# Encoder block on one core: branch A's exponentials left in PSUM, the first token block's keys regrouped in blocks of 128, half of the final scalings placed later

## The chip, the cores and the metric

One Trainium2 chip, one of its cores. The metric is device time of one execution in microseconds (us); lower is better. The kernel before ran three times: 1910.77 us is the median (1910.61 to 1911.93).

## What is computed

One layer of a hybrid encoder over two token groups with the same weights: `x_sample` (512 tokens) and `x_prompt` (2048 tokens), width 1024. 16 learned meta tokens stand ahead of each group. Cut to what matters here:

```python
u = rms_norm(h, norm_g)
qa, ka, va, za, qb, kb, vb, zb, ga, gb = split(u @ w_in)          # 42 tiles of 128 output columns
# branch A, 8 heads of 64: the tokens are a grid 64 wide; a query sees 8 rows x 16 columns and 16 meta keys
logits = concat([s_win * scale + bias, s_meta * scale]);  p = softmax(logits);  o_a = p @ v
# branch B, 8 query heads and 2 key heads: +-128 tokens and the meta keys, with a sink in the denominator
merged = sigmoid(ga) * ((o_a * silu(za)) @ w_proj_a) + sigmoid(gb) * ((o_b * silu(zb)) @ w_proj_b)
y = rms_norm(h + merged @ w_out, final_g)                          # meta tokens dropped
```

Everything is float32. A matrix product is made of three: each operand is split in a high part that TensorE's float32r holds and a low remainder, and high x high, high x low and low x high are added up (`mm3`, L134).

## The kernel before

The 2560 tokens are 5 windows of 512 (w = 0 is the sample, w = 1 to 4 the prompt). The first half, up to about 990 us, makes the input projection: window 4 tile by tile (`alone`, L679), the two pairs of windows by a seven-product scheme (`pairs`, L786). What the attention needs is written to DRAM: queries, keys, values, gates. The values of branch A go to `va_d`, ordered by blocks of 8 grid columns (`put_v`, L611); the meta values go to `vrow_d` (`put_v_meta`, L622), which is zeroed first from the tile `zr` (L625 to L630, run in the first half when the meta values of head pair 0 are ready). In this half TensorE's and SyncE's (SP's) order is that of the program; SP issues nearly all DMAs, one after the other.

The second half runs window by window: branch A's attention (32 units, `unit_a`, L980), then branch B's (`unit_b`, L1057). A unit is one head and one group g of 16 query columns, that is 128 queries. It goes through five steps that the main loop interleaves, so that four units are under way at a time:

1. loads (SP).
2. scores: two matmuls into a PSUM bank `s` of the pool `ps_s` (2 banks); VectorE (DVE) adds the bias and takes the maximum (`scores_max`, L950); ScalarE (ACT) writes the exponentials to the SBUF tile `pr`, regrouped by blocks of 8 columns, and sums them (`exps`, L959).
3. `normalise` (L967): `pr` times the inverse sum, in place; on ACT for g = 1, on DVE for the other three groups.
4. TensorE transposes `pr` block by block into a bank `tp` of the pool `ps_p` (3 banks); ACT and DVE split it in `ph` and `pl`.
5. TensorE multiplies `ph` and `pl` by the values into the bank `oa` (lists `A_ORDER` and `A_PRODUCTS`, L63 and L64). A block holds 8 columns of all key rows and one more row for the meta keys: 8 x (rows + 1) keys. In window 0 there are 8 rows, so a block has 72 keys; a head has 3, 4, 4 and 3 blocks to transpose in its four groups and 0, 6, 4 and 6 products.

Between these steps TensorE takes "dense" work in small pieces (`phases`, L1356): while branch A of window w runs, `dense_pb(w - 1)` and the first half of `dense_out(w - 1)`; while branch B runs, the second half of `dense_out(w - 1)`, `dense_pa(w)` and, filled in between, `dense_fin(w - 1)` (L1247). The last makes the RMSNorm factor `rbs` and then multiplies the eight result tiles `hT` by it on GpSimd (POOL), each followed by its store. In window 0 the dense work is the gate columns of window 4 (`gate`, L281). In this half TensorE's order is the program's; the other engines' order is the scheduler's. POOL also makes the low parts of the weights (`split_part`, L188, through `lo_eng`), POOL's share of `dense_pb` (L1219 and L1223) and `y` and its low part (`y_split`, L973).

Between the halves, `open_weights` (L937) sets `lo_eng` to POOL and splits the first weights of the second half; `prep_last(False)` (L299) makes window 4's operand `u` (L316 on ACT, L317 on DVE); and `finals` (L1396) are the last three sums of the seven-product scheme, on DVE, read out of PSUM banks that the second half's pools take over.

Of the kernel before, what the change touches and what calls it, by code (L numbers as in the profile page):

```python
# [70 lines left out]

def v_block(b):

    return b % 2 * 4 + b // 2
# [13 lines left out]
def encoder_block(ctx: ExitStack, tc: tile.TileContext, xT, x_end, w_in, w_pa, w_pb, w_o, norm_g, final_g,  # L88
# [15 lines left out]
    va_d = [dt(f"va{p}", [2, TOK // GRID_W * 8, 8, P]) for p in range(4)]  # L104
    vrow_d = [dt(f"vrow{p}", [8, 8, 2, P]) for p in range(4)]
# [192 lines left out]

    def prep_last(meta):  # L299
# [6 lines left out]
        for k in range(0, KT, 2):  # L306
# [601 lines left out]
    with tc.tile_pool(name="sp", bufs=1, reuse_waits="tile") as sp:  # L908
# [6 lines left out]
        next(steps)  # L915
        begun = beside(firsts, raws, wts, (own, (9, 14)), 0, steps, [2, 20, 27, *(28 + 27 * i // 10 for i in range(16))])
# [20 lines left out]
    def open_weights():  # L937
        nonlocal weights
        lo_eng[0] = nc.gpsimd
# [27 lines left out]
    def normalise(pr, rd, on_act=False):  # L967
        if on_act:
            nc.scalar.mul(pr, pr, rd)
        else:  # L970
            nc.vector.tensor_scalar(pr, pr, rd, None, ALU.mult)

    def y_split(br, w, p, y32, eng=nc.gpsimd):  # L973
# [4 lines left out]
        eng.tensor_sub(yl[:, p, :], y32, f32(yh[:, p, :]))  # L978

    def unit_a(w, p, h, g, sh):  # L980
# [17 lines left out]
        if g == 0:  # L998
# [5 lines left out]
            move(v[8:kb], va_d[p][h, t0 // 8 : t0 // 8 + kb - 8])  # L1004
            move(v[:8], vrow_d[p][:, :, h])
# [7 lines left out]
        s = ps_s.tile([P, WTOK], F32, tag="s", name="s")  # L1013
# [12 lines left out]
        for i, b in enumerate(A_ORDER[g]):  # L1026
# [369 lines left out]
    for fn in finals:  # L1396
        fn()
# [167 lines left out]
```

## Time and profile before

| | |
|---|---|
| median of 3 runs | 1910.77 us |
| the profiled execution's own time | 1908.84 us |
| its span (first to last instruction) | 1906.5 us |
| TensorE busy | 1878.5 us (99%) |
| VectorE busy | 1320.3 us (69%) |
| ScalarE busy | 1147.6 us (60%) |
| GpSimd busy | 731.9 us (38%) |
| DMA | 423.78 MB, 222 GB/s over the span |

How to read it: the page and the views describe the profiled execution, whose own time is the span and 2.3 us around it. Matmuls overlap in the pipeline, so the duration of one is longer than the distance from its start to the next one's start; the distance is what a matmul costs. "Idle before" an instruction is time in which its engine had nothing to run, and the name behind the arrow is what ended it.

### The profile page before, as it was taken

The page shows a single profiled execution, that of the slowest core. Times are in us where ns is not written, and L with a number is a line of the kernel's source. Part 1 is how long each engine was busy: PE and PEld are TensorE (multiplying, and loading weights), DVE is VectorE, ACT ScalarE, POOL GpSimd, SP SyncE. Part 2 cuts the span into 40 slices and gives each one's busy share as a digit, 9 for nine tenths or more (in the row PEclk, how much of TensorE's full clock was granted, in tenths as well). Part 3 has the DMA queues.
Part 4 walks back from the last instruction along what each step waited for, and adds up shares of the span by engine and source line. Part 5 has one row for each costly group of instructions (what it writes and reads, how often), then busy time and mean ns, then how long its engine had stood idle before and what let it go on. Part 6 is the DMA issues. An engine that isn't in the chain of part 4 may idle for free.

```text
span 1906.5 us, 29720 instructions
## 1 busy us (share of the span) xinstructions
PE 1878.5 (99%) x9925; PEld 1599.4 (84%) x9925; DVE 1320.3 (69%) x2887; ACT 1147.6 (60%) x2515; POOL 731.9 (38%) x556
## 2 busy tenths in 40 slices
PE   8999999999999999999999999999999999999998
PEld 6998888888888888888878888888888888888886
DVE  8886455556477544445457788878987887888874
ACT  6454443434464444444356787797788788878932
POOL 2005342323103232323223335655844773585420
PEclk9999999999999999999999999999999999999999
DMA  7667554645296765644368877977986996697473
GB/s 261 218 190 293 175 198 165 218 174 177 83 353 218 239 210 194 194 138 160 105 207 289 254 217 261 294 223 242 319 270 185 307 316 217 197 326 252 124 289 141
DMA packets 223760, 423.78 MB, mean 222 GB/s; under 512 B 49640, under 2 KB 90808, under 8 KB 222072
## 3 DMA queue, kind: packets, MB, share of 16 engines
q1 hardware_dynamic: 223320, 421.88, 66.8%
q8 instruction: 79, 1.29, 0.3%
q14 instruction: 73, 0.60, 0.1%
q10 hardware_dynamic: 288, 0.01, 0.0%
HBM read 303.07 MB, written 118.74 MB: 221 GB/s over the span
## 4 chain that ended last, share of the span: by engine, by line
PE 75%; DVE 9%; ACT 6%; DMA 5%; issue 3%; POOL 2%; SPq 0%; ACTq 0%; DVEq 0%; POOLq 0%
PE pa L762 21%; PE pe L762 10%; PE pc L762 5%; PE mm L135 4%; PE mm L137 4%; PE mm L136 4%; PE tp L1027 2%; PE pso L137 2%; PE pso L135 2%; PE pso L136 2%; PE tp L1129 1%; PE oa L1044 1%; PE oa L1042 1%; DVE s L953 1%; DMA wo<-wos 1%
## 5 line engine op out<-in xcount | busy, mean ns | idle before, releaser
L190 POOL TENSOR_TENSOR wt<-wraw,wt 128x512 fp32r<-128x512 f32 x164 | 215.4, 1331 | 288.2 <-ACT wt L189 288.1
L762 PE MATMUL pa<-u,wt 128*128 128x512 f32 x1008 | 242.9, 390 | 0.0
L762 PE MATMUL pa<-u,x 128*128 128x512 f32 x984 | 237.8, 390 | 0.0
L189 ACT CAST wt<-wraw 128x512 fp32r<-128x512 f32 x312 | 177.9, 620 | 73.8 <-PE mm L137 37.6
L762 PEld LDWEIGHTS pa<-u,wt 128*128 128x128 f32 x1008 | 188.7, 188 | 39.0
L762 PEld LDWEIGHTS pa<-u,x 128*128 128x128 f32 x984 | 183.9, 188 | 38.1
L733 POOL TENSOR_TENSOR s<-wraw,raw 128x512 f32<-128x512 f32 x40 | 57.9, 1447 | 271.7 <-DVE x L190 271.7
L135 PE MATMUL mm<-u,wt 128*128 128x512 f32 (+2 forms) x416 | 151.6, 364 | 7.3 <-ACT u L316 7.3
L728 POOL TENSOR_TENSOR s<-raw 128x512 f32<-128x512 f32 x40 | 60.0, 1500 | 253.3 <-DMA raw<-in_w_in_dram 137.0
L136 PE MATMUL mm<-u,wt 128*128 128x512 f32 (+2 forms) x416 | 147.5, 355 | 1.5 <-DVE u L317 1.5
L137 PE MATMUL mm<-u,wt 128*128 128x512 f32 (+2 forms) x416 | 147.5, 355 | 0.8 <-DVE wt L190 0.8
L190 DVE TENSOR_TENSOR wt<-wraw,wt 128x512 fp32r<-128x512 f32 x148 | 104.6, 746 | 61.6 <-ACT wt L189 61.5
L762 PE MATMUL pe<-u,wt 128*128 128x512 f32 x504 | 121.9, 391 | 0.0
L762 PE MATMUL pc<-u,wt 128*128 128x512 f32 x504 | 121.1, 389 | 0.0
L1031 DVE TENSOR_TENSOR pl<-tp,ph 128x512 fp32r<-128x512 f32 (+7 forms) x160 | 98.8, 617 | 24.0 <-ACT ph L1030 22.3
L762 PE MATMUL pe<-u,x 128*128 128x512 f32 x480 | 115.3, 389 | 0.0
L960 ACT ACTIVATE pr<-s,nm 128x384 f32<-128x384 f32 (+5 forms) x160 | 91.3, 571 | 37.9 <-DVE nm L953 35.4
L762 PEld LDWEIGHTS pc<-u,wt 128*128 128x128 f32 x504 | 94.6, 188 | 19.6
L762 PEld LDWEIGHTS pe<-u,wt 128*128 128x128 f32 x504 | 94.2, 188 | 19.4
L741 POOL TENSOR_TENSOR s<-wraw,s 128x512 f32<-128x512 f32 x40 | 52.9, 1322 | 146.2 <-DVE wt L190 146.2
L1030 ACT CAST ph<-tp 128x512 fp32r<-128x512 f32 (+7 forms) x160 | 84.7, 529 | 38.7 <-PE tp L1027 36.5
L135 PE MATMUL pso<-mh,wt 128*128 128x512 f32 x256 | 107.1, 418 | 0.0
(238 smaller groups left out, 5050.7 us busy)
## 6 DMA issues: line engine op xcount, KB each, us to landing
wraw<-in_w_in_dram SPq DMA_DIRECT2D x86, 512.0 KB
qa<-evq SPq DMA_DIRECT2D x20, 1024.0 KB
raw<-in_w_in_dram SPq DMA_DIRECT2D x40, 512.0 KB
q<-qa SPq DMA_DIRECT2D x20, 1024.0 KB
wraw<-in_w_o_dram SPq DMA_DIRECT2D x32, 512.0 KB
kbt<-kb SPq DMA_DIRECT2D x32, 384.0 KB
qb<-evq SPq DMA_DIRECT2D x20, 512.0 KB
ka<-evk SPq DMA_DIRECT2D x20, 512.0 KB
```

Of the source, the lines that this page charges most:

```text
L135: nc.tensor.matmul(ps, wh, uh, start=first, stop=False)
L136: nc.tensor.matmul(ps, wh, ul, start=False, stop=False)
L137: nc.tensor.matmul(ps, wl, uh, start=False, stop=last)
L189: nc.scalar.copy(h, r)
L190: low[0] = (eng or lo_eng[0]).tensor_sub(l, r, f32(h)).ins
L728: eng.tensor_add(s1, a21, a22)
L733: eng.tensor_sub(s3, a11, a21)
L741: eng.tensor_sub(s4, a12, s2)
L762: nc.tensor.matmul(ps, wt[:, a, s], u[:, b, kk, :], start=first and kk == 0 and i == 0, stop=kk == 3 and i == 2, skip_group_check=True)
L960: nc.scalar.activation(out, s, AF.Exp, bias=nm, scale=-1.0, accum_out=sm)
L1030: nc.scalar.copy(ph_[:kb, a], tb)
L1031: nc.vector.tensor_sub(pl_[:kb, a], tb, f32(ph_[:kb, a]))
```

## The change

- **Exponentials in PSUM.** For branch A, `exps` writes back into the bank of the scores, in its order, instead of into `pr`. `normalise` reads that bank and writes `pr`, regrouped. The bank is held until then. Every third unit takes its score bank from `ps_p` (the pool of the transposes), the others from `ps_s`. Branch B keeps its form.
- **Window 0's key blocks.** `pr` holds the 16 meta probabilities (normalised by a second small instruction in each unit) and then the 64 keys of each 8-column block without a gap. It is cut in blocks of 128 keys, some of them overlapping (`A0_BLOCKS`): 2, 3, 3 and 2 to transpose in the four groups, and 0, 4, 4 and 4 products (`A0_PRODUCTS`). The values of window 0 get an array of their own, `va0_d`, laid out in six such blocks of up to 128 rows; `put_v` stores into it with four DMAs for each head pair where there were two, `put_v_meta` with three more, and a unit loads it with two DMAs as before.
- **Zeros.** A function `zero_rows` sets `zr` and stores zeros into `vrow_d` (4 DMAs) and `va0_d` (8 DMAs). It runs at the start, behind the loads of the first operands; the 4 DMAs in `put_v_meta` are gone.
- **Final scalings.** For windows 0, 1 and 2, `dense_fin` scales and stores the first four tiles `hT`; the other four are scaled and stored during the next `dense_pb`, behind its fourth step. Window 3's stay together.
- **Between the halves.** `lo_eng` becomes POOL only after the first weights of the second half are split, so DVE makes the low parts of those; and the DVE instructions of `finals` are queued behind the last L317 of `prep_last`.

The diff, cut to its core:

```diff
+A0_BEGIN = ((16, 0), (16, 0), (16, 0), (0, 192))
+A0_BLOCKS = (((0, 0), (80, 1)), ((16, 2), (144, 4), (0, 6)), ((16, 5), (0, 7), (144, 9)), ((0, 10), (80, 11)))
+A0_PRODUCTS = ((),
+               (("h", 0, P, 1, (0, 1)), ("h", 4, 80, 0, (0,)), ("l", 4, 80, 0, (0,)), ("l", 0, P, 1, (0, 1))),
+               (("h", 1, P, 4, (1, 2)), ("l", 1, P, 4, (1, 2)), ("h", 5, 80, 6, (1, 2)), ("l", 5, 80, 6, (1, 2))),
+               (("h", 2, P, 9, (2, 3)), ("h", 3, P, 11, (3,)), ("l", 3, P, 11, (3,)), ("l", 2, P, 9, (2, 3))))
...
+    va0_d = [dt(f"va0{p}", [2, P, 6, P]) for p in range(4)]
...
-                nc.vector.scalar_tensor_tensor(ul[:, k + j, :WTOK], xt[:, j, :], g, f32(h), ALU.mult, ALU.subtract)
+                scaled[0] = nc.vector.scalar_tensor_tensor(ul[:, k + j, :WTOK], xt[:, j, :], g, f32(h), ALU.mult,
+                                                           ALU.subtract).ins
...
-        if br == "a":
+        if br == "a" and w == 0:
+            for rows, k, y, b in (slice(64, P), slice(0, 3), 0, 0), (slice(0, 64), slice(1, 4), 64, 0), \
+                    (slice(64, P), slice(3, 4), 48, 3), (slice(0, 64), slice(0, 1), N_META, 4):
+                n = k.stop - k.start
+                move(va0_d[p][:, y : y + 64, b : b + n].rearrange("g p k f -> p g k f"), vn[rows, :, k])
+        elif br == "a":
...
+    def zero_rows():
+        zr = ev.tile([P, WTOK], F32, tag="t", name="zr", bufs=3)[:, :P]
+        nc.vector.memset(zr, 0.0)
+        for d, v in zip(vrow_d, va0_d):
+            move(d.rearrange("c b g f -> (c b g) f"), zr)
+            move(v[:, :48, 3].rearrange("g p f -> p g f"), zr[:48, None, :].broadcast_to([48, 2, P]))
+            move(v[:, N_META:80, 5].rearrange("g p f -> p g f"), zr[:64, None, :].broadcast_to([64, 2, P]))
...
-            if p == 0:
-                zr = ev.tile([P, WTOK], F32, tag="t", name="zr", bufs=3)[:, :P]
-                nc.vector.memset(zr, 0.0)
-                for d in vrow_d:
-                    move(d.rearrange("c b g f -> (c b g) f"), zr)
+            for y, b in (P - N_META, 3), (0, 4), (0, 5):
+                move(va0_d[p][:, y : y + N_META, b].rearrange("g p f -> p g f"), vm[:, :, 0])
...
         next(steps)
+        zero_rows()
         begun = beside(firsts, raws, wts, (own, (9, 14)), 0, steps, [2, 20, 27, *(28 + 27 * i // 10 for i in range(16))])
...
     def open_weights():
         nonlocal weights
-        lo_eng[0] = nc.gpsimd
         weights = Weights(srcs)
...
-            move(v[8:kb], va_d[p][h, t0 // 8 : t0 // 8 + kb - 8])
-            move(v[:8], vrow_d[p][:, :, h])
+            if w == 0:
+                move(v[:, :4], va0_d[p][h, :, :4])
+                move(v[:80, 4:6], va0_d[p][h, :80, 4:])
+            else:
+                move(v[8:kb], va_d[p][h, t0 // 8 : t0 // 8 + kb - 8])
+                move(v[:8], vrow_d[p][:, :, h])
...
-        s = ps_s.tile([P, WTOK], F32, tag="s", name="s")
+        turn[0] += 1
+        s = (ps_p.tile([P, WTOK], F32, tag="tp", name="s") if turn[0] % 3 == 0 else
+             ps_s.tile([P, WTOK], F32, tag="s", name="s"))
...
-        pr = at.tile([P, 2 * HALF], F32, tag="pr", name="pr", bufs=3)[:, :WTOK]
-        sm = sums_of()[:, :1]
-        exps(pr[:, :n].rearrange("p (b r c) -> p r b c", b=nb, c=8), sv.rearrange("p r (b c) -> p r b c", c=8), nm, sm)
-        yield
-        normalise(pr[:, :n], inverse(sm), on_act=g == 1)
+        sm = sums_of()[:, :1]
+        exps(s[:, :n], s[:, :n], nm, sm)
+        yield
+        pr = at.tile([P, 2 * HALF], F32, tag="pr", name="pr", bufs=3)[:, :WTOK]
+        rd = inverse(sm)
+        x, r0 = (A0_BEGIN[g][0], 1) if w == 0 else (0, 0)
+        normalise(pr[:, x : x + nb * 8 * (R - r0)].rearrange("p (b r c) -> p r b c", b=nb, c=8),
+                  sv[:, r0:].rearrange("p r (b c) -> p r b c", c=8), rd, on_act=g == 1)
+        if w == 0:
+            x, m0 = A0_BEGIN[g][1], META_COLS[(0, 0, 1, 2)[g]] - c0
+            normalise(pr[:, x : x + N_META], sv[:, 0, m0 : m0 + N_META], rd, on_act=g == 1)
...
-    def dense_fin(w):
+    def dense_fin(w, fs):
...
-        for f in range(KT):
+        yield from final_scale(w, range(fs))
+
+    def final_scale(w, fs):
+        for f in fs:
             hT = acc["h", w, f]
             with tc.issue_after(low[0]):
-                nc.gpsimd.tensor_mul(hT, hT, rbs)
+                nc.gpsimd.tensor_mul(hT, hT, acc["r", w])
...
-                yield from dense_pb(w - 1)
+                pb = dense_pb(w - 1)
+                yield from islice(pb, 4)
+                yield from with_fill(pb, final_scale(w - 2, range(KT // 2, KT)) if w > 1 else iter(()))
                 yield from dense_out(w - 1, range(0, 4))
...
-            yield from with_fill(pa, dense_fin(w - 1))
+            yield from with_fill(pa, dense_fin(w - 1, KT if w == NWIN - 1 else KT // 2))
...
+    lo_eng[0] = nc.gpsimd
...
-    for fn in finals:
-        fn()
+    with tc.issue_after(scaled[0]):
+        for fn in finals:
+            fn()
```

## Rows read from the trace of the kernel before

**Rows 1.** The page, first part: busy time, share of the span and instructions of each engine.

```profile
PE 1878.5 (99%) x9925; PEld 1599.4 (84%) x9925; DVE 1320.3 (69%) x2887; ACT 1147.6 (60%) x2515; POOL 731.9 (38%) x556
```

**Rows 2.** The view of waits, TensorE alone: who waited for whom; total us, times, longest us.

```profile
PE mm L135 <- ACT u L316: 7.3, 1, 7.3
PE psb L136 <- POOL yb L978: 2.9, 3, 1.3
PE psa L135 <- ACT rbs L1255: 2.6, 3, 0.9
PE mm L136 <- DVE u L317: 1.5, 1, 1.5
PE tp L1027 <- DVE pr L971: 1.4, 5, 0.5
```

**Rows 3.** The view by windows: the stretch from 985 to 1080 us (window 0's branch A) and from 1300 to 1400 us (end of window 1's branch B, then most of window 2's branch A): length, busy us and count of each engine, granted TensorE clock, DMA busy share, GB/s.

```profile
985.00:1080.00 95.00, 93.32 (x550) 79.82 (x550) 71.80 (x188) 62.98 (x152) 38.18 (x30) 1.00 0.84 272
1300.00:1400.00 100.00, 97.65 (x582) 83.34 (x582) 88.45 (x215) 75.92 (x173) 70.40 (x55) 1.00 0.92 298
```

**Rows 4.** The timeline of TensorE in window 0's branch A: start us, us, engine, line, operation, tile, shape, count.

```profile
997.33 0.49 PE L1027 MATMUL tp<-ident,pr 128*72 128x128 f32 x3
997.57 0.48 PE L135 MATMUL mm<-u,wt 128*128 128x512 f32 x1
...
999.27 0.60 PE L1027 MATMUL tp<-ident,pr 128*72 128x128 f32 x4
999.62 0.48 PE L135 MATMUL mm<-u,wt 128*128 128x512 f32 x1
...
1003.63 0.28 PE L1044 MATMUL oa<-pl,v 72*64 72x256 f32 x1
1003.75 0.29 PE L1015 MATMUL s<-kd,q 128*128 128x288 f32 x1
```

**Rows 5.** The view of groups by shape, TensorE: all transposes of window 0's branch A (72 keys each): busy us, mean ns of one, idle before.

```profile
L1027 PE MATMUL tp<-ident,pr 128*72 128x128 f32 x112 | 17.4, 272 | 0.0
```

**Rows 6.** The view of the tile `pr` (duration ns: least, median, most; first and last start; forms), and the view of groups by shape for VectorE (busy us, mean ns of one, idle before): branch A's normalisation in SBUF, and the bias-and-maximum instruction, which reads and writes PSUM, at 384 columns.

```profile
L971 DVE TENSOR_SCALAR pr<-pr,rd x120: 315/504/1608, 995.1 to 1741.0; 128x384 f32<-128x384 f32 x40, 128x288 f32<-128x288 f32 x24, 128x216 f32<-128x216 f32 x16, 128x512 f32<-128x512 f32 x16
...
L971 DVE TENSOR_SCALAR pr<-pr,rd 128x384 f32<-128x384 f32 x40 | 31.6, 791 | 0.6
L953 DVE CUSTOM_DVE_ANT_0 s<-s,ba 128x384 f32<-128x384 f32 x48 | 26.6, 554 | 3.4 <-PE s L1016 3.4
```

**Rows 7.** The timeline of all engines around 1336 us: GpSimd, two normalisations, TensorE.

```profile
1334.49 2.73 POOL L190 TENSOR_TENSOR wt<-wraw,wt 128x512 fp32r<-128x512 f32 x2 [0.49 <-ACT wt L189]
1334.61 1.45 DVE L971 TENSOR_SCALAR pr<-pr,rd 128x512 f32<-128x512 f32 x1
...
1336.12 0.66 PE L1027 MATMUL tp<-ident,pr 128*128 128x128 f32 x4 [0.39 <-DVE pr L971]
...
1339.45 0.42 DVE L971 TENSOR_SCALAR pr<-pr,rd 128x384 f32<-128x384 f32 x1
```

**Rows 8.** The timeline of GpSimd at the end of window 1's branch B, and the TensorE instruction that waited for the last of it.

```profile
1317.30 5.05 POOL L1259 TENSOR_TENSOR hT<-hT,rbs 128x512 f32<-128x512 f32 x4 [2.46 <-ACT rbs L1255]
...
1326.24 5.27 POOL L1259 TENSOR_TENSOR hT<-hT,rbs 128x512 f32<-128x512 f32 x4
...
1337.17 1.29 POOL L978 TENSOR_TENSOR yb<-y,yb 128x512 fp32r<-128x512 f32 x1
...
1338.51 0.50 PE L136 MATMUL psb<-yb,wt 128*128 128x512 f32 x1 [0.81 <-POOL yb L978]
```

**Rows 9.** The timeline of all engines around 1316 us: a normalisation, the copy of `rbs` on ScalarE, and TensorE's wait for the bank that it frees.

```profile
1312.31 1.38 DVE L971 TENSOR_SCALAR pr<-pr,rd 128x384 f32<-128x384 f32 x1
...
1316.64 0.57 ACT L1255 COPY rbs<-rs_rb 128x512 f32<-128x512 f32 x1
...
1317.27 0.50 PE L135 MATMUL psa<-ya,wt 128*128 128x512 f32 x1 [0.93 <-ACT rbs L1255]
```

**Rows 10.** The timeline of all engines between the halves: the first four L317, the last two, the matmul that waited for the first of those, the last of `finals`' reads of PSUM, and the second half's first scores.

```profile
980.65 2.74 DVE L317 SCALAR_TENSOR_TENSOR u<-xt,ng,u 128x512 fp32r<-128x512 f32 x4 [8.47 <-ACT u L316]
...
988.52 1.40 DVE L317 SCALAR_TENSOR_TENSOR u<-xt,ng,u 128x512 fp32r<-128x512 f32 x2
989.32 0.51 PE L136 MATMUL mm<-u,wt 128*128 128x512 f32 x1 [1.48 <-DVE u L317]
...
990.18 0.68 DVE L263 TENSOR_TENSOR eva<-pb,u 128x512 f32<-128x512 f32 x1
...
990.96 0.34 PE L1015 MATMUL s<-kd,q 128*128 128x216 f32 x1 [0.20 <-PE mm L137]
```

**Rows 11.** The start: the view of the tile `zr` (issue time of its stores in ns on SP: least, median, most), and the timeline: an early memset, SP's issue of the fifth weights, their cast, and the sums that the next two windows' operands hang on.

```profile
L131 SPq DMA_DIRECT2D vrow<-zr x4: 417/570/1135, 104.1 to 106.5; - x4
...
0.95 0.06 DVE L339 MEMSET sq<- 128x5 f32 x1
...
19.01 0.43 SPq L131 DMA_DIRECT2D wraw<-in_w_in_dram  x1
...
28.75 1.13 ACT L189 CAST wt<-wraw 128x512 fp32r<-128x512 f32 x2
...
41.89 1.92 PE L410 MATMUL fin_v<-ones,rsp 128*128 128x1 f32 x16 [0.23 <-DVE rsp L405]
```

**Rows 12.** The view of waits, SP alone: the longest of those for GpSimd's low part in `dense_pb`; total us, times, longest us.

```profile
SPq L131 <- POOL ml L1223: 34.5, 20, 4.4
```

More of the change, by code (lines that the diff above doesn't have):

```diff
@@ L965, in inverse, with normalise @@
         return rd
-    def normalise(pr, rd, on_act=False):
+    def normalise(out, pr, rd, on_act=False):
         if on_act:
-            nc.scalar.mul(pr, pr, rd)
+            nc.scalar.mul(out, pr, rd)
         else:
-            nc.vector.tensor_scalar(pr, pr, rd, None, ALU.mult)
+            nc.vector.tensor_scalar(out, pr, rd, None, ALU.mult)
     def y_split(br, w, p, y32, eng=nc.gpsimd):
@@ L978, in y_split @@
         eng.tensor_sub(yl[:, p, :], y32, f32(yh[:, p, :]))
+    turn = [0]
     def unit_a(w, p, h, g, sh):
@@ L1018, in unit_a @@
         nm = scores_max(s, n, bias[:, b0 : b0 + n])
+        sm = sums_of()[:, :1]
+        exps(s[:, :n], s[:, :n], nm, sm)
+        yield
         pr = at.tile([P, 2 * HALF], F32, tag="pr", name="pr", bufs=3)[:, :WTOK]
-        sm = sums_of()[:, :1]
-        exps(pr[:, :n].rearrange("p (b r c) -> p r b c", b=nb, c=8), sv.rearrange("p r (b c) -> p r b c", c=8), nm, sm)
-        yield
-        normalise(pr[:, :n], inverse(sm), on_act=g == 1)
+        rd = inverse(sm)
[5 more added lines that the diff above has]
+            normalise(pr[:, x : x + N_META], sv[:, 0, m0 : m0 + N_META], rd, on_act=g == 1)
         yield
         tp = ps_p.tile([P, WTOK], F32, tag="tp", name="tp")
-        for i, b in enumerate(A_ORDER[g]):
-            nc.tensor.transpose(tp[:kb, i * P : (i + 1) * P], pr[:, b * kb : (b + 1) * kb], ident)
-        a = slice(A_FIRST[g], A_FIRST[g] + 2 * nb - 1, 2)
-        tb = tp[:kb, : nb * P].rearrange("p (b t) -> p b t", t=P)
+        if w == 0:
+            kb, blocks = P, A0_BLOCKS[g]
+            products = A0_PRODUCTS[g]
+        else:
+            blocks = [(b * kb, A_FIRST[g] + 2 * i) for i, b in enumerate(A_ORDER[g])]
+            products = [(part, v_block(b), kb, x, gs) for part, b, x, gs in A_PRODUCTS[g]]
+        for i, (x, _) in enumerate(blocks):
+            nc.tensor.transpose(tp[:kb, i * P : (i + 1) * P], pr[:, x : x + kb], ident)
+        a = slice(blocks[0][1], blocks[-1][1] + 1, blocks[1][1] - blocks[0][1])
+        tb = tp[:kb, : len(blocks) * P].rearrange("p (b t) -> p b t", t=P)
         nc.scalar.copy(ph_[:kb, a], tb)
@@ L1035, in unit_a @@
         o = sh.get("o")
-        for i, (part, b, x, gs) in enumerate(A_PRODUCTS[g]):
-            vb = v[:kb, v_block(b), :]
+        for i, (part, b, m, x, gs) in enumerate(products):
+            vb = v[:m, b, :]
             cols = slice(gs[0] * P, (gs[-1] + 1) * P)
-            src = (ph_ if part == "h" else pl_)[:kb, x : x + len(gs)].rearrange("p b t -> p (b t)")
+            src = (ph_ if part == "h" else pl_)[:m, x : x + len(gs)].rearrange("p b t -> p (b t)")
             if part == "h":
@@ L1043, in unit_a @@
             else:
-                nc.tensor.matmul(o[:64, cols], vb[:, :64], src, start=False, stop=(g, i) == (3, 5),
+                nc.tensor.matmul(o[:64, cols], vb[:, :64], src, start=False, stop=(g, i) == (3, len(products) - 1),
                                  skip_group_check=True)
@@ L1253, in dense_fin @@
         rb = spread(ps_d, "d", dg, P, 4)
[L1254 removed]
+        rbs = acc["r", w] = pools["d"].tile([P, WTOK], F32, tag="rbs", name="rbs", bufs=1)
         nc.scalar.copy(rbs, rb)
[L1256 removed]
+        yield from final_scale(w, range(fs))
+    def final_scale(w, fs):
+        for f in fs:
             hT = acc["h", w, f]
             with tc.issue_after(low[0]):
[L1259 removed]
+                nc.gpsimd.tensor_mul(hT, hT, acc["r", w])
             dst = outT_s if w == 0 else outT_p
```

4 lines of the change are left out of this document (2 added, 2 removed).

## Prediction

> **What bounds the kernel now.** I read first the page's busy shares [rows 1]: TensorE runs 1878.5 us of a span of 1906.5. So a gain must come from one of two places: fewer TensorE instructions, or the 28 us in which it is idle. The view of waits for TensorE [rows 2] says where these are. 7.3 us are the start, which the change leaves alone; 8.4 us are four groups of waits that the change can touch: for GpSimd's `yb` (2.9), for the copy of `rbs` (2.6), for `u` between the halves (1.5), for `pr` (1.4). The view by windows [rows 3] shows the rest: even in window 0's branch A TensorE is busy 93.3 of 95 us, at a granted clock of 1.00, with VectorE at 72; in window 2's branch A VectorE has 88 of 100 and GpSimd 70. Work taken from VectorE, ScalarE or GpSimd is therefore worth only the waits that it ends.
>
> **The first block's matmuls.** Before, a head has 14 transposes (112 for 8 heads, [rows 5]); after, 2 + 3 + 3 + 2 = 10. The timeline gives the price [rows 4]: three transposes take 997.57 - 997.33 = 0.24 us until the next matmul, four take 999.62 - 999.27 = 0.35, so one more costs 0.11 (0.35 / 4 = 0.09 is the lower bound). 32 fewer: 3.5 us (2.8 to 3.5). Products fall from 16 to 12 a head; the four that go, two each in groups 1 and 3, all have 256 columns, whose distance is 1003.75 - 1003.63 = 0.12 us [rows 4]: 32 x 0.12 = 3.8 us. A block of 128 keys where there were 72 has more rows and no more columns, and I cost that at nothing. This is work of the engine that sets the end: **-7.3 us**. ScalarE and VectorE also lose four block copies and four subtractions of 128 columns a head, which hides the new small instruction for the meta probabilities (no row; I bound it between nothing and the 0.42 us of a free normalisation of 384 columns [rows 7], 24 of them on VectorE, 10 us at most against the 23 us that it has idle in that stretch [rows 3]).
>
> **Normalisation out of PSUM.** In SBUF its 120 instructions on VectorE take from 0.32 to 1.61 us [rows 6]. The timeline tells why the same form varies: at 1334.61 a 512-column one takes 1.45 us while GpSimd runs until 1337.2; at 1339.45, with GpSimd at rest, 384 columns take 0.42 [rows 7]. At 384 columns the mean is 0.791 [rows 6]. The trace has no such instruction that reads PSUM. Its bounds are 0.42 us (free, from SBUF) and 0.554 (the bias-and-maximum at 384 columns, which reads and writes PSUM [rows 6]); I take 0.55, the nearer kind. The mean falls by 0.24 us, and the 1.4 us that TensorE waited for late `pr` should go: -1.4 (0 to -1.4).
>
> One rule speaks against this. The Trainium skill, VectorE: DVE Perf Modes, section Why PSUM operands drop a tier, says that a PSUM operand loses the two-port mode, so a float32 multiplication by a scalar runs at half the rate. By that alone VectorE would get 0.55 for 0.42, 120 x 0.13 = 16 us more. The same skill, SBUF - State Buffer, section SBUF: two separate sides, says that the two-port mode needs a port that GpSimd holds for a whole instruction; the trace agrees, with 1.45 us beside 0.42. By the first rule alone the step loses, by both it gains.
>
> ScalarE's exponentials have the same columns and a PSUM target; I cost the difference at nothing, since ScalarE has a quarter of its time free [rows 3].
>
> The score bank is now held from the scores to the normalisation, one turn of the loop longer. With every third bank from `ps_p`, a bank comes back three units later, while the normalisation is one unit later, so I expect no wait. If the cover failed, each unit would pay (third rival).
>
> **The copy of `rbs`.** TensorE waits for the bank that this copy frees: 0.93 us at 1317.27 [rows 9]. ScalarE is not slow there; its exponentials ahead of the copy wait for VectorE, which spent 1.38 us on one normalisation from 1312.31. With 0.55 in its place the copy is some 0.8 us earlier. Of 2.6 us in three places I take -1.9 (0 to -2.6).
>
> **Final scalings moved.** At the end of branch B, GpSimd runs 5.27 us of scalings shortly ahead of the last `yb` [rows 8], and TensorE waits 0.81 us for that. Four of these eight leave this place, 5.2 us of GpSimd's queue; their four stores leave SP's queue there too. -2.4 of 2.9 (0 to -2.9). They go into `dense_pb`, where GpSimd is at its fullest (70 of 100 us, [rows 3]) and its low part `ml` already holds SP up, 4.4 us at the longest [rows 12]; behind SP's wait lie the loads for units four turns ahead. 4 x 1.3 = 5.2 us of new work in each of three windows meets idle time of GpSimd in between; I put **+0.5** us on it (0 to +4).
>
> **Between the halves.** The last two L317 come behind three sums of `finals`, and TensorE waits 1.48 us for the first [rows 10]. With the order turned round, this wait goes. What is late next: the scores start at 990.96, just behind the end (990.86) of the sum that reads the last old bank. VectorE's work is the same, so that sum can only move up by the gaps. I take -1.0 (-0.5 to -1.7). Two low parts of the first weights go from GpSimd to VectorE; they cost about what two L317 cost (1.4 us at most), and VectorE is idle for 8.5 us ahead of the first L317 [rows 10], so nothing.
>
> **Zeros.** 12 stores at 0.57 us [rows 11] put 6.8 us on SP between the second half of the first operands (in the queue ahead of them, so not delayed) and the fifth weights, whose issue goes from 19.0 to about 26. Their cast ran at 28.75, 9.7 us behind the issue [rows 11], and how much of that was slack no row shows: the cast is put off by 0 to 6.8 us. ScalarE works in order, and behind this cast come squares that lead to the sums at 41.89, which already waited 0.23 us [rows 11]. TensorE has its next weights until then, so I take **+0.6**, near the lower bound (0 to +6.8). The memset itself is free: an early memset ran at 0.95 us, when VectorE had nothing [rows 11]. The other 20 DMAs that SP gets (3 and 2 more for each of four head pairs) fall into a half in which no wait of TensorE for a DMA is among the long ones [rows 2]: nothing.
>
> **The sum.** -7.3 - 1.4 - 1.9 - 2.4 - 1.0 = -14.0; +0.5 + 0.6 = +1.1; net -12.9 us. The profiled execution took 1908.84 us (its span and 2.3 around it): 1895.9. It is 1.9 us under the median of the runs, so I add that: **1897.9 us**.
>
> **Rivals.**
> *Only the matmul work goes.* The waits are ended in their old place and come back: GpSimd in `dense_pb` is 5.2 us later, the last `ml` of a window is needed by the first `dense_out` product, and SP is held up longer. For: GpSimd's 70 us [rows 3] and the 34.5 us of SP [rows 12]. Against: it has gaps, and a normalisation out of PSUM no longer competes with it. Price: -7.3 and nothing else, 1908.84 - 7.3 + 1.9 = 1903.4; about 1902 to 1907.
> *The zeros come too early.* The fifth weights and then the squares are late, by half the bound: +3.4 instead of +0.6, 1900.7. For: the sums that already wait [rows 11]. Against: the cast ran 9.7 us behind the issue.
> *Slower: the held bank.* VectorE, 88% busy, does the normalisation late, and TensorE waits at the scores or the transposes of the unit behind. The mechanism is the lengthening from 0.42 to 0.55 that no blocking hides: if each of the 160 units then held TensorE by 0.13 us, the sum is -12.9 + 21 = +8, 1919 us. It decides from 12.9 / 160 = 0.08 us a unit on. Against: mean 0.791 now, so most are shortened, and three units between uses.
> *The stretch is not TensorE's.* Window 0's branch A moves 272 GB/s at a DMA share of 0.84 [rows 3]; if its loads set its length, the 7.3 us saved come back as waits: 1905.2. Against: 298 GB/s at 0.92 elsewhere [rows 3], and no such wait now.
>
> **How the numbers follow.** Forecast 0.60 (all of it faster), only matmuls 0.20, zeros 0.08, the stretch bound by DMA 0.06, held bank 0.06. A change of 0.2%, 3.8 us, is about what a measurement of this kernel can tell from none: faster is below 1907.0, slower above 1914.6. Only matmuls gives 0.18 faster and 0.02 same; DMA 0.04 and 0.02; the bank 0.02 same and 0.04 slower. Together 0.90, 0.06, 0.04. The lower end takes every bound at its best, -7.3 - 1.4 - 2.6 - 2.9 - 1.7 = -15.9, to 1894.9, and some of the spread of the runs (1.3 us): 1893.5. The upper end takes in the rivals at 1903.4 and 1905.2 and a little of `dense_pb`: 1906.
>
> **What would show it.** Right: 80 transposes and 96 products in window 0's branch A, its stretch about 7 us shorter; the normalisations at 384 columns near 0.55 us with little spread; no wait for `yb` and `pr`, little for `rbs`; first scores some 1 us earlier against the start of the half. Wrong: waits of TensorE for `s`, for `wt` or `ml` in `dense_pb`, for DMA in window 0; or a gap ahead of 42 us. The prediction fails if new waits in the second half add up to more than 6 us.

## Result and profile after

The changed kernel takes 1913.62 us (median of 20 runs, 1909.82 to 1919.01), the kernel before 1909.84 (20 runs, 1907.72 to 1913.22): a ratio of 1.0019, 95% interval 1.0012 to 1.0025. By the ratio it is slower by 3.6 us, where 12.9 us less were forecast. The profiled execution took 1913.96 us with a span of 1911.8.

The page's first part [rows 1]: TensorE is busy for 4.5 us less, but the span is 5.3 us longer, so its idle time (span less busy time) went from 28.0 to 37.8 us.

```profile
PE 1874.0 (98%) x9861; PEld 1594.8 (83%) x9861; DVE 1301.3 (68%) x2913; ACT 1143.8 (60%) x2523; POOL 719.0 (38%) x554
```

The view of waits, TensorE alone (total us, times, longest us), against [rows 2]. The waits for `yb`, `pr` at `tp` and half of those for `rbs` are gone, as forecast (those for `pr` in this kernel, but not in all that normalise out of PSUM; see why the prediction was wrong). In their place stand new ones: branch A's products for `pl` (4.0), branch B's scores (L1158) for branch A's `pr` and `ph` (2.3 and 1.0), its transposes for `pms` (1.0), `psb` for `sgb` (1.4 and 1.3), the first scores for an eviction (2.0), window 0's `psa` for `ta` (2.0, where it was 0.3), and more for weights at the start (2.5, where it was 0.8).

```profile
PE oa L1093 <- DVE pl L1080: 4.0, 2, 3.7
PE mm L150 <- DVE wt L203: 2.5, 2, 1.6
PE s L1158 <- DVE pr L999: 2.3, 2, 1.4
PE s L1052 <- DVE eva L276: 2.0, 1, 2.0
PE psa L148 <- DVE ta L1252: 2.0, 1, 2.0
PE psb L148 <- DVE sgb L1358: 1.4, 1, 1.4
PE psb L148 <- DVE sgb L1267: 1.3, 2, 1.0
PE psa L148 <- ACT rbs L1305: 1.2, 2, 0.6
PE s L1158 <- ACT ph L1079: 1.0, 1, 1.0
PE tp L1178 <- DVE pms L1196: 1.0, 1, 1.0
```

**The first block** does what it says. The view of groups by shape for window 0's branch A [rows 5] has 80 transposes for 112, and TensorE's first scores and branch B's first products are 96.6 us apart (992.5 to 1089.1) where they were 103.0 (991.0 to 1094.0): 6.4 us less.

```profile
L1076 PE MATMUL tp<-ident,pr 128*128 128x128 f32 x80 | 14.0, 272 | 0.0
```

Branch B's first products, in the timeline of TensorE before, then after:

```profile
1093.97 0.28 PE L1153 MATMUL ob<-ph,vb 128*128 128x256 f32 x1
...
1089.14 0.28 PE L1202 MATMUL ob<-ph,vb 128*128 128x256 f32 x1
```

**The normalisation out of PSUM** is shorter and steadier, as forecast. The view of groups by shape for VectorE, and of the tile `pr` (ns: least, median, most), against [rows 6]: at 384 columns the mean is 615 ns where it was 791, and the longest of all forms is 753 where it was 1608. The small one for the meta keys, which had no row, is 226 ns.

```profile
L999 DVE TENSOR_SCALAR pr<-s,rd 128x384 f32<-128x384 f32 x40 | 24.6, 615 | 0.7
...
L999 DVE TENSOR_SCALAR pr<-s,rd 128x16 f32<-128x16 f32 x24 | 5.4, 226 | 0.0
```

```profile
L999 DVE TENSOR_SCALAR pr<-s,rd x144: 224/540/753, 996.4 to 1743.2; 128x384 f32<-128x384 f32 x40, 128x16 f32<-128x16 f32 x24, 128x192 f32<-128x192 f32 x16, 128x288 f32<-128x288 f32 x16
```

**The longest new wait** is in window 3's branch A. The timeline, all engines: GpSimd runs the four moved scalings from 1515.38, with `ml` behind them; SP issues the four stores (1519.80), and one load of `sgb` only at 1528.03. VectorE, in order, stands 5.64 us for a load of `sgb` with the `pl` of an attention unit behind it, and TensorE stands 3.74 us for that `pl`.

```profile
1515.38 5.04 POOL L1312 TENSOR_TENSOR hT<-hT,rbs 128x512 f32<-128x512 f32 x4
...
1519.80 4.64 SPq L144 DMA_DIRECT2D out_dram<-hT  x4
...
1521.63 1.29 POOL L1272 TENSOR_TENSOR ml<-sgb,mh 128x512 fp32r<-128x512 f32 x1
...
1528.03 0.32 SPq L144 DMA_DIRECT2D sgb<-gb  x1
...
1534.98 0.69 DVE L1267 TENSOR_TENSOR sgb<-psb,sgb 128x512 f32<-128x512 f32 x1 [5.64 <-DMA sgb<-gb]
1535.59 0.55 DVE L1080 TENSOR_TENSOR pl<-tp,ph 128x384 fp32r<-128x384 f32 x1
...
1536.19 0.58 PE L1093 MATMUL oa<-pl,v 128*64 128x128 f32 x2 [3.74 <-DVE pl L1080]
```

The view by windows there (columns as in [rows 3]): the third number from the end is the granted clock. TensorE, idle for most of the wait, has 0.51 (the lower of the two levels, 1.2 GHz, for nearly the whole stretch) in the next 5 us and 0.81 in the 5 behind them. So, as an estimate from these rows, the wait costs about 3.81 x 0.49 + 5.00 x 0.19 = 2.8 us of its busy time on top.

```profile
1530.00:1535.00 5.00, 2.45 (x14) 1.88 (x12) 0.02 (x1) 0.21 (x2) 1.66 (x2) 1.00 1.02 368
1535.00:1540.00 5.00, 3.81 (x14) 3.42 (x15) 4.23 (x11) 3.71 (x8) 2.71 (x3) 0.51 0.79 294
1540.00:1545.00 5.00, 5.00 (x27) 4.21 (x26) 4.12 (x11) 2.97 (x8) 4.88 (x5) 0.81 1.05 291
```

**Between the halves** (timeline against [rows 10]) the wait for `u` is gone, and the first scores wait 1.98 us for the sum that reads an old bank (`eva<-pb`). It ends at 992.43 where it ended at 990.86; the first `pa` of the first half comes 1.5 us later too (127.2 for 125.7), so the whole of that shift is as old as the start:

```profile
991.75 0.68 DVE L276 TENSOR_TENSOR eva<-pb,u 128x512 f32<-128x512 f32 x1
...
992.53 0.34 PE L1052 MATMUL s<-kd,q 128*128 128x216 f32 x1 [1.98 <-DVE eva L276]
```

### The profile page after: what moved, and what is told of

It reads as the page before. It is cut to its first block, busy times and chain, and to the rows that moved or that the text cites. A ratio compares the mean times of both kernels' runs of the same rounds, so it can differ in the third digit from the quotient of the medians.

```text
span 1911.8 us, 29713 instructions
## 1 busy us (share of the span) xinstructions
PE 1874.0 (98%) x9861; PEld 1594.8 (83%) x9861; DVE 1301.3 (68%) x2913; ACT 1143.8 (60%) x2523; POOL 719.0 (38%) x554
## 4 chain that ended last, share of the span: by engine, by line
PE 77%; DMA 7%; DVE 7%; ACT 4%; POOL 2%; issue 2%; SPq 1%; DVEq 0%; ACTq 0%; POOLq 0%
PE pa L790 21%; PE pe L790 10%; PE pc L790 5%; PE mm L150 4%; PE mm L148 4%; PE mm L149 4%; PE pso L149 2%; PE pso L150 2%; PE pso L148 2%; PE tp L1076 2%; PE tp L1178 2%; DMA sgb<-gb 1%; DMA wo<-wos 1%; PE oa L1093 1%; PE oa L1091 1%
## 5 line engine op out<-in xcount | busy, mean ns | idle before, releaser
L203 POOL TENSOR_TENSOR wt<-wraw,wt 128x512 fp32r<-128x512 f32 x162 | 209.0, 1310 | 295.5 <-ACT wt L202 295.5
L1079 ACT CAST ph<-tp 128x384 fp32r<-128x384 f32 (+6 forms) x160 | 81.6, 510 | 49.3 <-PE tp L1076 47.2
L1080 DVE TENSOR_TENSOR pl<-tp,ph 128x384 fp32r<-128x384 f32 (+6 forms) x160 | 95.0, 594 | 21.5 <-ACT ph L1079 18.8
L981 DVE CUSTOM_DVE_ANT_0 s<-s,ba 128x384 f32<-128x384 f32 (+5 forms) x160 | 86.8, 543 | 28.7 <-PE s L1053 27.1
```

The source lines that it names most:

```text
L203: low[0] = (eng or lo_eng[0]).tensor_sub(l, r, f32(h)).ins
L981: nc.vector.tensor_tensor_reduce(s[:, :n], s[:, :n], bias, -1.0, 3.0e38, ALU.add, ALU.min, nm)
L1079: nc.scalar.copy(ph_[:kb, a], tb)
L1080: nc.vector.tensor_sub(pl_[:kb, a], tb, f32(ph_[:kb, a]))
```

## Experiments

Two theories came out of this trace. **H, the held bank**: at the turn from branch A to branch B the score bank, which now lives one step longer, holds TensorE up. **G, GpSimd's block**: the four scalings in `dense_pb` delay `ml`, the loads of `sgb` and, with them, VectorE and TensorE. Rivals: the zeros or the new stores at the start; the order between the halves; the mere sum of GpSimd's time. The changed kernel, "after" from here on, is at 1.0019. Each ratio is to executions of before that ran beside it, in four groups (e1 to e4, e5 to e8, e9 to e12, e13 to e16); a difference of two ratios is given in us of 1910.

| run | ratio to before | 95% interval |
|---|---|---|
| e1 after, scalings back | 0.9998 | 0.9989 to 1.0008 |
| e2 after, zeros back | 1.0057 | 1.0043 to 1.007 |
| e3 after, windows 1 to 4 in SBUF | 0.9992 | 0.9983 to 1.0 |
| e4 after, scalings and zeros back | 1.0024 | 1.0015 to 1.0033 |
| e5 first block, zeros, order alone | 0.9979 | 0.997 to 0.9989 |
| e6 as e5, without the order | 0.9981 | 0.9972 to 0.999 |
| e7 scalings moved alone | 1.001 | 1.0001 to 1.0018 |
| e8 PSUM alone | 1.000 | 0.9991 to 1.0009 |
| e9 after, turn repaired | 0.9988 | 0.998 to 0.9997 |
| e10 after, moved tiles not stored | 1.001 | 1.0001 to 1.0019 |
| e11 after, moved tiles not scaled | 0.9978 | 0.9966 to 0.9989 |
| e12 e9 with scalings back | 0.9967 | 0.9955 to 0.9978 |
| e13 e9, scalings in `dense_out` | 0.9959 | 0.9947 to 0.9971 |
| e14 e12 without the order | 0.9978 | 0.9968 to 0.9987 |
| e15 PSUM alone, turn repaired | 0.9977 | 0.9969 to 0.9986 |
| e16 e9, scalings untied from the weight split | 0.9964 | 0.995 to 0.9977 |

### One part undone (e1 to e4)

e1 puts the scalings back, e2 the zeros, e4 both; in e3 windows 1 to 4 write their exponentials to SBUF again and take all score banks from `ps_s`.

```diff
 e1, e4
-                yield from with_fill(pb, final_scale(w - 2, range(KT // 2, KT)) if w > 1 else iter(()))
+                yield from with_fill(pb, iter(()))
-            yield from with_fill(pa, dense_fin(w - 1, KT if w == NWIN - 1 else KT // 2))
+            yield from with_fill(pa, dense_fin(w - 1, KT))
 e2, e4
         next(steps)
-        zero_rows()
 ...
         if br == "a":
+            if p == 0:
+                zero_rows()
             for y, b in (P - N_META, 3), (0, 4), (0, 5):
 e3: for w > 0 as in the kernel before
+            exps(pr[:, :n].rearrange("p (b r c) -> p r b c", b=nb, c=8),
+                 sv.rearrange("p r (b c) -> p r b c", c=8), nm, sm)
+            yield
+            normalise(pr[:, :n], pr[:, :n], inverse(sm), on_act=g == 1)
```

> The changed kernel with all eight final scalings of a window back in dense_fin; all else as changed. Theory S (the scalings and their four stores, which the scheduler puts in one block on GpSimd and ahead of the loads on SP in dense_pb, cost the time): the 3.74 us wait for pl in window 3's branch A and the granted clock of 0.51 behind it go, the waits for yb (2.9 us) come back; some 6 us under the changed kernel, ratio to the kernel before about 0.9985. Theory P (normalising out of PSUM changes the order on VectorE and holds the score banks, and this costs the time): as the changed kernel or worse by 2 us, ratio 1.002 to 1.003. Theory Z (the early zeros): ratio 1.002.

> The changed kernel with zero_rows called in put_v_meta for head pair 0, where the zeros were stored before; all else as changed. Theory Z: the first matmul of the seven-product scheme comes back from 127.2 to 125.7 us and the waits at 36.5, 57.1 and 59.5 us shrink; 1.5 us less, ratio 1.0011. Theories S and P: this start is worth 1.5 us at most, and the loss in windows 2 to 4 stays, ratio 1.001 to 1.002.

> The changed kernel with branch A's exponentials of windows 1 to 4 in SBUF as before (regrouped by ScalarE, normalised in place, score banks of ps_s alone); window 0 stays in PSUM, with its blocks of 128; zeros and scalings as changed. Theory P: the loss behind 1140 us goes, ratio about 0.998. Theory S: the wait for sgb and pl in dense_pb stays and VectorE's normalisations wait for GpSimd's block of four scalings, ratio 1.002 or more. Theory Z: ratio 1.002.

> The changed kernel with both the final scalings and the zeros back where they were. If the two losses are separate, it gains what the two other runs gain, under theory S about 7.5 us on the changed kernel, ratio 0.998; under theory P 1.5 us, ratio 1.001.

Moving the scalings costs 0.0021 (4.0 us) here, and in e1, without it, there is still no long wait for `yb` (three of 0.3 us at most): in this kernel the normalisation out of PSUM ends these waits without the move, to which the prediction credited them (2.4 us). e3, which keeps the move and undoes PSUM, is 5 us faster than after: PSUM, with the score banks that it holds, costs time in this kernel. The zeros are no culprit but a gain: with them back in their old place the time is 7.3 us above after (e4 over e1: 5.0). TensorE's timeline in e2 shows why: with the new stores of meta values in the same place, weights of the pairs come late, which no wait of after shows at that point.

```profile
134.60 1.08 PE L792 MATMUL pa<-u,wt 128*128 128x512 f32 x2 [3.23 <-ACT wt L202]
137.15 3.35 PE L792 MATMUL pa<-u,wt 128*128 128x512 f32 x7 [1.47 <-DVE wt L203]
```

### One part alone (e5 to e8)

e5 is after with e1's edit and e3's; e6 also undoes the order:

```diff
     def open_weights():
         nonlocal weights
+        lo_eng[0] = nc.gpsimd
 ...
-    with tc.issue_after(scaled[0]):
-        for fn in finals:
-            fn()
+    for fn in finals:
+        fn()
```

e7 is before with the move of the scalings as in the change's diff, e8 before with the score banks, the exponentials and the normalisation as in it, in all five windows (the key blocks of window 0 stay as before).

> The first block's new keys with its zeros at the start and the order between the halves; the scalings are back in dense_fin, and windows 1 to 4 have their exponentials in SBUF as before. If the moved scalings and the PSUM exponentials of windows 1 to 4 are what was lost, separately, this is the best so far: the 6.4 us that window 0's branch A lost less the 0.5 of the start, and the waits of before in windows 1 to 4 (yb, rbs, pr); some 1904 us, ratio 0.997. If instead any new order on VectorE brings new waits in windows 1 to 4, ratio 0.999 to 1.001.

> As the kernel with the first block alone, and the two edits between the halves undone too: the low parts of the first weights of the second half on GpSimd, and finals not queued behind L317. If that order only trades the wait for u (1.5 us) for one of the scores for the sum out of the old bank (2.0 us), the same time within 0.1%. If it gained the 1.0 us of the prediction, 0.05% more than the kernel with it. If the early order was a loss, less.

> The kernel before with the moved final scalings alone. Theory S (scalings in dense_pb cost more than the waits for yb that they end): slower, ratio 1.002 to 1.004, with waits for sgb or pl in dense_pb and the store of hT ahead of the loads on SP. As the prediction had it: -2.4 + 0.5 us, ratio 0.999.

> The kernel before with the exponentials in PSUM alone, in all five windows, with the blocks of 72 keys in window 0. As the prediction had it: -1.4 for pr and -1.9 for rbs, ratio 0.998. Theory H (held bank at the turn from branch A to branch B, where a score of branch B needs the bank of one of the last units of branch A): new waits of 0.9, 1.4 and 1.0 us for the scores of branch B at the ends of branch A, and waits for tp at the units of dense_pb, ratio 1.000 to 1.002.

The first block with its zeros and stores is worth 0.0021 (4.0 us) alone. The order shows no gain (0.9979 and 0.9981 beside each other, with intervals too wide to tell 1.0 us from nothing): in e6 TensorE waits 1.44 us for `u` and not for the eviction. The move costs 1.9 us alone, though the waits for `yb` are gone: TensorE now waits for `pr` (5.2 us, where it was 1.4, the longest 3.0) and for `pl` (2.3). PSUM alone gives nothing, though it ends most of the waits for `yb` (0.8 left of 2.9) and half of those for `rbs`. The view of waits of e8 shows what it gets in exchange. The transposes wait longer for `pr` (2.9 us, where it was 1.4); branch B's scores wait for branch A's `pr` and `ph` at the turn to branch B (at 1571.45 the longest, 1.45 us); and the wait for `pms` comes at the turn back, at 1652.6, 3.7 us behind the first scores of window 4's branch A:

```profile
PE tp L1032 <- DVE pr L971: 2.9, 3, 1.5
PE s L1114 <- DVE pr L971: 2.4, 2, 1.5
...
PE s L1114 <- ACT ph L1035: 1.0, 1, 1.0
PE tp L1134 <- DVE pms L1152: 1.0, 1, 1.0
```

### The held bank (e9, e12, e15)

Branch B takes its score banks from `ps_s` alone (L1155 of after). Branch A counts its units through all windows, 32 to a window, and 32 is no multiple of 3: in windows 0, 1, 3 and 4 the last unit (turns 32, 64, 128, 160) sits in a bank of `ps_s`, in window 2 (turn 96) in one of `ps_p`. After has its waits at L1158 for `pr` and `ph` in windows 1, 3 and 4 and none in window 2. It has none in window 0 either, so such a bank makes the wait possible, not certain. The wait for `pms` belongs to the other seam: branch B's last transposes take banks of `ps_p` (L1171), and window 4's first unit (turn 129) holds one of these. That this bank is its cause is argued from the turns.

The repair takes the turn from the unit's place in its window, so that the last unit always has a `ps_p` bank:

```diff
-        turn[0] += 1
-        s = (ps_p.tile([P, WTOK], F32, tag="tp", name="s") if turn[0] % 3 == 0 else
+        s = (ps_p.tile([P, WTOK], F32, tag="tp", name="s") if (8 * p + 4 * h + g) % 3 == 1 else
              ps_s.tile([P, WTOK], F32, tag="s", name="s"))
```

e9 is after with it, e12 has e1's edit besides, e15 is e8 with it.

> The changed kernel with another choice of every third score bank: counted within the window so that the window's last unit of branch A always has a bank of ps_p, and not one that the first scores of branch B need. Theory H (held bank at the turn to branch B): the waits of those scores at 1230.8 (0.92), 1575.1 (1.43) and 1743.9 (0.99 us) go, as window 2, whose last unit's turn is a multiple of three, has none now; 3.3 us less, ratio about 1.000. Rival (VectorE is simply late there, whatever the bank): the same waits under another name, ratio 1.002.

> The changed kernel with the scalings back in dense_fin and the score banks chosen so that the last unit of a window has one of ps_p. Theory H: the run with the scalings back (ratio 0.9998) less 3.3 us, 0.998. Without H: 0.9998.

> The kernel before with the exponentials kept in PSUM in all five windows and the repaired turn, nothing else of the change. Theory H (with the turn as in the change, the bank held to the end of branch A eats what the normalisation gives back, which is why that part alone measured 1.0000): ratio 0.997 to 0.9985, that is 3 to 6 us less than before, and no wait of branch B's first scores for pr, ph or pms over 0.9 us. Rival (the normalisation from PSUM gives nothing, and the repaired turn only worked together with the rest): 0.9993 to 1.0007.

H holds: all three repairs gain, after to e9 0.0031 (5.9 us), e1 to e12 0.0031, e8 to e15 0.0023 (4.4 us), each pair with intervals apart, and in e9, e12 and e15 no wait of branch B's scores for `pr` or `ph` and none for `pms` is left in the view of waits. These waits were 4.3 us in after; the repair gives other units a `ps_p` bank too, and where the rest of the 5.9 us comes from is not shown. The normalisation out of PSUM is worth its price once the bank is out of the way (e15, 0.9977). e12 beats both kernels.

### GpSimd's block: time, stores or place (e10, e11, e13, e16)

```diff
 e10: for the four moved tiles of a window no store;  e11: no multiplication (they are stored unscaled)
+            if scale:
                 with tc.issue_after(low[0]):
                     nc.gpsimd.tensor_mul(hT, hT, acc["r", w])
+            if store:
                 move(dst[f * P : (f + 1) * P, c0 : c0 + WTOK], hT)
 e13: on e9
-                yield from with_fill(pb, final_scale(w - 2, range(KT // 2, KT)) if w > 1 else iter(()))
-                yield from dense_out(w - 1, range(0, 4))
+                yield from pb
+                yield from with_fill(dense_out(w - 1, range(0, 4)),
+                                     final_scale(w - 2, range(KT // 2, KT)) if w > 1 else iter(()))
 e16: on e9
-            with tc.issue_after(low[0]):
+            with tc.issue_after(low[0]) if f < KT // 2 or w == NWIN - 2 else nullcontext():
```

> The changed kernel without the stores of the four result tiles that are scaled in dense_pb (windows 0 to 2): the multiplications stay on GpSimd, twelve stores of 256 KB are left out, so these parts of the output are not written. Theory D (the moved stores go from a stretch where the DMA engines have slack to branch A's, where they are busy to 1.0, and the loads of sgb behind them are late): as with the scalings back, ratio about 0.9997, and no wait for pl or sgb in dense_pb. Theory G (GpSimd's block of four multiplications): ratio 1.002, the waits stay.

> The changed kernel without the multiplications of those four tiles: they are stored in dense_pb unscaled, twelve multiplications on GpSimd are left out. Theory G: ratio about 0.9997. Theory D: ratio 1.002, the waits for sgb and pl stay.

> The kernel after with the repaired turn of the score banks (as in the run of 0.9988), and the four moved scalings filled in among the first output blocks of dense_out, behind the weight split's ml of the projection, in place of among the units of dense_pb. Theory P (the place: GpSimd's block of four stands ahead of ml and of sgb's additions in dense_pb): the cost of moving goes, ratio about 0.997 (as with the scalings back and the turn repaired, 0.9967), and TensorE has no wait over 2 us for VectorE's pl. Rival T (GpSimd's time at that point of the window as such, or the lateness of the stores, wherever they are put): 0.9988 or above, with new waits of the output's products (psa or pso) of about 1 us each.

> The kernel after with the repaired turn (0.9988), where the four scalings that were moved to dense_pb no longer stand in the order behind the weight split's last instruction: the scheduler may put each where GpSimd is free. Theory B (the block: tied together they run as four in a row, 20 us, with ml and sgb's additions behind them): they spread, ratio 0.9968 to 0.998. Rival T (their 20 us of GpSimd in that stretch cost as such): 0.9988 or more, with the same four in a row or with waits for sgb elsewhere.

Without the multiplications the time is 7.8 us under after, without the stores only 1.7, with intervals that overlap. e11 alone doesn't say why, since it also spares GpSimd work that e1 still does. e13 does: it runs the same 32 scalings and is 5.5 us faster than e9, with no wait for `pl` over 0.5 us. So it is the place of the scalings (and of their stores, which move with them), not GpSimd's time. GpSimd's timeline in e13 shows the block behind the last `sgb` addition and ahead of the last `ml` only:

```profile
1368.34 1.29 POOL L1271 TENSOR_TENSOR ml<-sgb,mh 128x512 fp32r<-128x512 f32 x1 [0.27 <-ACT mh L1270]
1371.17 1.28 POOL L1267 TENSOR_TENSOR sgb<-sgb,ta 128x512 f32<-128x512 f32 x1
1373.66 5.04 POOL L1311 TENSOR_TENSOR hT<-hT,rbs 128x512 f32<-128x512 f32 x4
1378.64 1.28 POOL L1271 TENSOR_TENSOR ml<-sgb,mh 128x512 fp32r<-128x512 f32 x1
```

That has a price of its own, a wait for `ml`, which is 0.6 us in after and more here. The view of waits of e13:

```profile
PE pso L149 <- POOL ml L1271: 3.7, 3, 1.5
```

e16 did not do what was expected of it. Untied, the four did not spread: the scheduler ran all eight in a row right behind `rbs`, at the end of branch B, so that it is another form of e12 (0.9964 beside 0.9967), not a test of spreading.

```profile
1313.25 10.06 POOL L1311 TENSOR_TENSOR hT<-hT,rbs 128x512 f32<-128x512 f32 x8 [2.22 <-ACT rbs L1304]
```

### The order, once more (e14)

e12 with the order undone as in e6.

> The kernel after with the repaired turn and the final scalings back in dense_fin (measured 0.9967), and the order between the halves undone (finals queued without waiting for the last gate's scaling). Theory: the order trades a wait for u of 1.4 us against one for the first eviction of 2.0 us and is worth nothing: 0.9967 within 0.001, the wait for eva at the first scores gone and one of about 1.4 us for u back. Rival (the order gives what the prediction put on it, 1.0 us): 0.9972 or above.

This came out at the rival's number. But e12 was measured beside other runs of before, its interval (0.9955 to 0.9978) overlaps that of e14, and e5 beside e6 shows no gain. The waits were traded as expected (1.49 us for `u`). Whether the order is worth up to 2 us in this version stays open.

## Why the prediction was wrong, by its own steps

- **The first block's matmuls, -7.3**: right in mechanism, 0.9 us short in size. The stretch lost 6.4 us. With the zeros and the order (e5) 4.0 us of it reach the end, without the order (e6) 3.6. A part goes to the later start (below), a part to a wait that comes with the shorter stretch: `psa` for `ta` at the end of window 0's branch B, 2.0 us in after, 0.8 to 1.5 in the other kernels with the new blocks, 0.3 at most in those with the old ones.
- **Normalisation out of PSUM, -1.4**: right on VectorE, wrong on the wait. 0.615 us stands above both bounds taken for it (0.42 and 0.554): -0.18 us each where -0.24 was put. The rule that spoke against the step (the Trainium skill, VectorE: DVE Perf Modes, section Why PSUM operands drop a tier: a PSUM operand loses the two-port mode) agrees in direction with a single instruction, 0.615 for 0.42; over all 40 of 384 columns in before the mean from SBUF was 0.791. The waits for `pr` did not end by this step: where it is made and the scalings are in `dense_fin`, they are longer than before (1.4), 2.9 us in e8, 4.0 in e1, 3.9 in e12, 4.3 in e15. The timeline of e12 shows how: VectorE, in order, stands 2.68 us for a load of `sgb`, and the normalisation behind it is late.

```profile
1525.77 0.69 DVE L1266 TENSOR_TENSOR sgb<-psb,sgb 128x512 f32<-128x512 f32 x1 [2.68 <-DMA sgb<-gb]
...
1527.04 0.61 DVE L999 TENSOR_SCALAR pr<-s,rd 128x384 f32<-128x384 f32 x1
...
1527.80 0.52 PE L1075 MATMUL tp<-ident,pr 128*128 128x128 f32 x3 [1.92 <-DVE pr L999]
```

In after such a stand ends in `pl` and not in `pr` (the longest new wait). e15 gains 4.4 us all the same, and no view shows where: its waits for `yb` and `rbs` are 3.3 us shorter than before's and those for `pr` 2.9 us longer, and its traced execution (1908.81 us) is 3.1 us over the median of its runs.
- **"A bank comes back three units later ... so I expect no wait": this step failed.** It counted turns within branch A and forgot that the loop leaves branch A, where the next user takes from `ps_s` alone. Price 5.9 us in after (e9), 4.4 alone. The slower rival named the held bank, but as a cost in each of 160 units, from longer instructions; it was one wait in each of four places where the branches change (4.3 us in after's view of waits), which is another mechanism.
- **"Final scalings moved", -2.4 and +0.5 (0 to +4): mis-sized, and its gain was not its own.** Most of the waits for `yb` end with the PSUM normalisation by itself (e8, e1), so the move had almost nothing left to win. Its cost was 1.9 us alone (e7), 4.0 in after (e1), 5.5 against a place behind nearly all `ml` (e13). The prediction looked at GpSimd's share of the stretch (70 us of 100) and at SP, but not at what stands in order behind the late `ml`: the buffers of `sgb`, their loads, and VectorE, which carries branch A's `pl` in the same queue. The longest new wait shows this chain once; that it carries the whole cost is not shown. The rival "only the matmul work goes" had the place right and priced the waits as coming back, not as new ones.
- **The copy of `rbs`, -1.9**: half right, 1.4 us of 2.6 gone (also in e8; 1.0 to 1.1 in e12, e13 and e15).
- **Between the halves, -1.0**: no gain seen. The sum that reads the old bank did not move up against the rest, and the scores wait for it in place of `u`.
- **Zeros, +0.6**: the first `pa` comes 1.5 us later (127.2 for 125.7), within the bounds. These are single executions; the other kernels with the zeros at the start have it at 126.0 to 128.8, those with the start of before (e7, e8, e15) at 124.5 to 126.0. "The other 20 DMAs ...: nothing" holds only because the zeros had left that place (e2).

Put together from the ratios, e13 (0.9959) is 7.8 us faster than before: it has every part of the change, the turn repaired and the scalings in a better place. The bank takes 5.9 of this and the place of the scalings 5.5, which leaves after 3.6 us slower. The other 5.1 us to the forecast of 12.9 are only argued, from the waits: the order (1.0), the start (0.9), the block (0.9), and in e13 the wait for `ml` (3.1 more than in after). These come to 5.9 and do not divide the 5.1.

Not settled: how the 4 to 5.5 us of the scalings' place divide. The 3.74 us wait and the clock behind it are one case in one window; e9, which doesn't have it (its waits for `pl` come to 2.1 us, the longest 1.3), still loses 4.0 us to e12. Late loads of `sgb` are also not the moved scalings' alone. The view of waits for VectorE in `dense_pb`, in before, e8 (no scalings moved), after and e13:

```profile
DVE sgb L1218 <- DMA sgb<-gb: 0.2, 1, 0.2
DVE sgb L1223 <- DMA sgb<-gb: 8.3, 5, 2.6
DVE sgb L1267 <- DMA sgb<-gb: 10.9, 7, 5.6
DVE sgb L1266 <- DMA sgb<-gb: 3.6, 4, 1.8
```

It is 10.2 us in e7, where the scalings are moved and the normalisation stays in SBUF. In after without the moved stores (e10) it is 11.7 us, without the moved multiplications (e11) 8.8, so the moved block accounts for the longest of these waits rather than for their sum. Why the loads also come late once the normalisation reads PSUM was not tried.

## What to carry to other kernels

When a buffer is held longer, count its turns over the whole loop, above all at the seam where another user takes from only some of the buffers. A rotation that doesn't divide the units of a window can put the fault into some windows and not into others, and such a pattern is a sign to look for. When work is moved to an engine with idle time, look for what stands behind it in program order on the engines that wait for that engine's results; here the same 15 us of GpSimd (three blocks of 5) cost 5.5 us more ahead of the `ml` of a stretch than behind most of them. And before a gain is credited to one part of a change, ask whether another part ends the same wait by itself.

## What was not expected of the hardware

A normalisation of 16 columns out of PSUM takes 226 ns on VectorE, where 384 columns take 615: 389 / 368 = 1.06 ns a column, and some 209 ns that no column explains. But its neighbour starts before it ends. In VectorE's timeline of after, the next instruction comes 0.14 us behind the start of a small one and 0.53 us behind that of one of 384 columns (also the median of the 37 behind which VectorE had no idle time):

```profile
1027.42 0.23 DVE L999 TENSOR_SCALAR pr<-s,rd 128x16 f32<-128x16 f32 x1
1027.56 0.15 DVE L992 RECIPROCAL rd<-sm 128x1 f32<-128x1 f32 x1
...
1517.56 0.61 DVE L999 TENSOR_SCALAR pr<-s,rd 128x384 f32<-128x384 f32 x1
...
1518.09 0.55 DVE L1080 TENSOR_TENSOR pl<-tp,ph 128x384 fp32r<-128x384 f32 x1
```

So the 24 small ones for the meta keys, 5.4 us of busy time, hold VectorE up for some 24 x 0.14 = 3.4 us, an estimate from these rows. One wait of TensorE of 3.74 us was followed by a granted clock of 0.51 and 0.81, and so cost about 6.5 us by the estimate above. ScalarE's exponentials at 384 columns, which now go back to PSUM in the scores' order, are no longer than those into SBUF in regrouped order were; the view of groups by shape for ScalarE, before and after:

```profile
L960 ACT ACTIVATE pr<-s,nm 128x384 f32<-128x384 f32 x48 | 28.0, 583 | 10.4 <-DVE nm L953 8.3 <-DVE rd L964 1.6
...
L988 ACT ACTIVATE s<-s,nm 128x384 f32<-128x384 f32 x48 | 26.8, 559 | 2.4 <-DVE rd L992 1.4 <-DVE nm L981 0.7
```
